# First layer's feed-forward input as seven products of halves per gate/up pair, with the output product in groups of three tiles

## Chip, cores and metric

One NeuronCore of a Trainium2 chip. The metric is the device time of one execution in microseconds (us); three executions of the kernel before are the yardstick. All numbers below come from these times, from one profiled execution of the kernel before, and from the order of its instructions on each engine.

Engines: PE is TensorE (matmul), DVE VectorE, ACT ScalarE, POOL GpSimd, SP the queue from which all transfers are issued.

## What is computed

A two-layer backbone on 512 latent and 256 context tokens, 1024 channels wide. Each layer has three mixers, a gated merge, and a SwiGLU feed-forward block; the second layer's context tokens are not needed after its mixers, so its feed-forward block sees 512 tokens, the first layer's 768.

```python
def swiglu(h, w_in, w_out):
    gate, up = jnp.split(h @ w_in, 2, axis=-1)
    return (jax.nn.silu(gate) * up) @ w_out

for l in range(DEPTH):                       # DEPTH = 2, D_MODEL = 1024, FFN_HIDDEN = 2816
    ...
    hf = rmsnorm(x, norm_ffn[l]) * (1.0 + sc_f) + sh_f
    x = x + gt_f * swiglu(hf, w_ffn_in[l], w_ffn_out[l])
    if not last:
        hfc = rmsnorm(xc, norm_ffn[l]) * (1.0 + scc_f) + shc_f
        xc = xc + gtc_f * swiglu(hfc, w_ffn_in[l], w_ffn_out[l])
```

## The kernel before

Activations lie channel-first: a tile is 128 channels by 768 tokens (512 latent, then 256 context). Every float32 operand of a large matmul is split in a high part (a cast to the matmul's float32r type) and a low part (the rest), and a product is the sum of three passes: high by high, high by low, low by high (`gemm`, `sub`). A 1024-channel input is eight k-tiles, so one block of 128 output channels costs 8 x 3 matmuls of 512 columns (latent) and as many of 256 (context).

Weights come in blocks of 128 output channels. `run_items` keeps a list of items in program order, and for each one that has a weight block it loads the block (`load`, three buffers `wr`, L300), lets ACT cast the high part (`wh`, L323) and DVE subtract to get the low part (`wl`, L326), about one to two items ahead of the matmuls. Generators that are added with `add` (norms, and `ada_late`, which computes the second layer's adaLN vectors on DVE from 256 KB pieces `wad` at L513 and L515) are advanced by `tick` between matmuls. A scheduler then sets the final order on each engine, and each engine runs its own list strictly in order.

The feed-forward block is `ffn_items`. 22 pairs of a gate and an up block; each pair is two items. The gate product is evacuated by ACT with Silu (L1616), the up product is multiplied to it by DVE straight out of PSUM (L1620), and the result is split by ACT (L173) and DVE (L174). The pairs go in groups of 8, 8 and 6; after each group the output product (w_fo, 8 blocks) takes the group's tiles as k-tiles, and DVE adds it, scaled, to the residual (L1601). The first two pairs of layer 0 are done token set by token set, since the norm of the context tokens comes later. The last group's output product goes token set by token set, with the next norm behind it.

Pools: `base` holds 27 tiles "T" (16 of them the input's high and low parts, 8 the residual), the phase's pool has 23 tiles "T2". PSUM has three banks "g" and four "h" for products.

Of the kernel before, what the change touches and what calls it, by code (L numbers as in the profile page):

```python
# [22 lines left out]
KT = D // 128  # L23
# [8 lines left out]
ZS = ((13, 19), (10, 18))  # L32
LEVELS = (1, 2, 4, 8, 16, 32, 64)
FFN_GROUPS = ((0, 8), (8, 8), (16, 6))


AQ, AK, AV, GQ, GK, GV, GR, NQ, NK, NV = 0, 4, 5, 6, 8, 10, 14, 18, 22, 26
# [90 lines left out]


class Item:  # L130
    def __init__(self, fn, w=None, nk=0, raw=False):
        self.fn, self.w, self.nk, self.raw = fn, w, nk, raw


class Net:
    def __init__(self, ctx, tc, a, out, dbg=None):
        self.ctx, self.tc, self.nc, self.a, self.out = ctx, tc, tc.nc, a, out
        self.dbg = dbg
        self.items = []
# [149 lines left out]

    def run_items(self):  # L290

        ws = [n for n, it in enumerate(self.items) if it.w is not None]
        raw, split, early = {}, {}, set()
        st = {"d": 0, "s": 0, "q": 0, "lo": None}

        def load():
            while st["d"] < len(ws) and len([q for q in raw if q not in early]) < 3:
                it = self.items[ws[st["d"]]]
                t = self.base.tile([128, 1024], F32, tag="wr", name=self.nm("wr"), bufs=3)
                self.nc.sync.dma_start(t[:, :it.nk * 128], it.w)  # L300
                raw[st["d"]] = t
                st["d"] += 1

        def split_lo():
            f, st["lo"] = st["lo"], None
            if f:
                f()

        def split_hi(k):

            while st["s"] < len(ws) and st["s"] <= k:
# [10 lines left out]
                r = raw[q]  # L322
                self.nc.scalar.copy(hi[:, :n], r[:, :n])  # L323

                def lo_part(q=q, n=n, hi=hi, lo=lo, r=r):
                    self.nc.vector.tensor_tensor(out=lo[:, :n], in0=r[:, :n], in1=hi[:, :n].bitcast(F32), op=ALU.subtract)  # L326
                    del raw[q]
                    split[q] = (hi, lo)
                st["lo"] = lo_part
                st["s"] += 1  # L330
# [18 lines left out]
        self.preload = preload  # L349
        self.ahead, self.split_lo = ahead, lambda: (split_lo(), load())  # L350
        for it in self.items:
            if it.w is None:
                it.fn()
                continue
            q = st["q"]
            load()
            if not it.raw:
                split_lo()
                if q not in split:
                    split_hi(q)  # L360
# [1127 lines left out]
    def merge_items(self, l, x_src, ntok):  # L1488
        nc = self.nc
# [117 lines left out]
    def ffn_items(self, l, ntok):  # L1607
        nc = self.nc
# [23 lines left out]
        for gi, (t0, tn) in enumerate(FFN_GROUPS):  # L1632
# [5 lines left out]
            if lead and l < DEPTH - 1:  # L1638
                self.do(lambda: self.add(self.ada_late(l + 1)))
            for t in range(t0 + lead, t0 + tn):  # L1640
                pair(t, subs_of)
            w = lambda j: self.a["w_fo"][l, j][:, t0 * 128:(t0 + tn) * 128]
            if gi < len(FFN_GROUPS) - 1:
# [148 lines left out]
```

## Time and profile before

| what | value |
|---|---|
| median of 3 executions | 2516.41 us (2516.09 to 2519.16) |
| profiled execution, device time | 2517.52 us |
| its span, first to last instruction | 2515.7 us |
| mean granted TensorE clock | 0.993 |
| PE / DVE / ACT / POOL busy, share of span | 97% / 59% / 41% / 14% |

The span is 1.8 us shorter than the profiled execution's own time, which is 1.1 us above the median. A page of the profile gives busy time by engine, the span in slices, the chain of work that ended last, and the costliest groups of instructions. Matmuls overlap at their ends, so their rate is read from the distance between starts and not from their durations; the same holds, by a few hundredths of a microsecond, for DVE.

### The profile page before, as it was taken

The numbers are of one execution on the slowest core, as the hardware profiler recorded it, in microseconds if no ns is written. First come the engines' busy times: TensorE is split into PE (matmuls) and PEld (weight loads), VectorE is DVE, ScalarE is ACT, GpSimd is POOL, SyncE is SP. The second block draws the span as 40 slices with busy tenths as digits, with TensorE's granted clock in tenths as the row PEclk, the third lists the DMA queues.
The fourth block names the chain that finished last, engine by engine and source line by source line (L and its number), as shares of the span: only waits on it lengthen the run. The fifth ranks groups of instructions, "written<-read, shape, count | busy, mean of one in ns | idle before, by whom it ended". The sixth has DMA issues, their size and how long they took to land. (4 is left out here: it accounts for less than half of the span.)

```text
span 2515.7 us, 39662 instructions
## 1 busy us (share of the span) xinstructions
PE 2441.8 (97%) x15356; PEld 2068.8 (82%) x15356; DVE 1484.7 (59%) x3006; ACT 1043.1 (41%) x1723; POOL 345.9 (14%) x442
## 2 busy tenths in 40 slices
PE   6999999999999999999999998999999999999998
PEld 3777888988878888888888876777888879988887
DVE  5675457647667673544544587757657668533336
ACT  3543345546554452212212255535545656422223
POOL 1231113204203010000000011313212220000000
PEclk9999999999999999999999999999999999999999
DMA  6433542222247333323333351223332366433334
GB/s 233 137 128 116 180 125 82 86 82 61 68 146 257 126 118 96 122 93 103 123 94 104 122 172 64 89 97 112 102 92 74 106 225 190 149 99 94 96 93 122
DMA packets 123340, 300.53 MB, mean 119 GB/s; under 512 B 22288, under 2 KB 32272, under 8 KB 123152
## 3 DMA queue, kind: packets, MB, share of 16 engines
q1 hardware_dynamic: 123152, 298.00, 37.5%
q8 instruction: 121, 1.98, 0.3%
q14 instruction: 67, 0.55, 0.1%
HBM read 258.61 MB, written 29.57 MB: 115 GB/s over the span
## 5 line engine op out<-in xcount | busy, mean ns | idle before, releaser
L211 PE MATMUL g<-T,wh 128*128 128x512 f32 (+1 forms) x4672 | 1240.1, 353 | 2.8 <-ACT T L767 2.6
L211 PEld LDWEIGHTS g<-T,wh 128*128 128x128 f32 x4672 | 801.9, 190 | 118.4 <-issue 13.6
L211 PE MATMUL g<-T,wl 128*128 128x512 f32 (+1 forms) x2336 | 814.9, 349 | 0.4 <-DVE wl L326 0.4
L211 PE MATMUL h<-T,wh 128*128 128x512 f32 (+1 forms) x2624 | 660.2, 342 | 8.5 <-ACT T L168 7.4
L323 ACT CAST wh<-wr 128x1024 fp32r<-128x1024 f32 (+2 forms) x355 | 344.6, 972 | 688.3 <-PE h L211 258.5
L326 DVE TENSOR_TENSOR wl<-wr,wh 128x1024 fp32r<-128x1024 f32 (+2 forms) x355 | 406.8, 1146 | 300.4 <-ACT wh L323 286.4
L211 PEld LDWEIGHTS h<-T,wh 128*128 128x128 f32 x2624 | 450.9, 189 | 75.7 <-ACT T L168 9.1
L211 PEld LDWEIGHTS g<-T,wl 128*128 128x128 f32 x2336 | 443.2, 190 | 57.5 <-issue 0.6
L211 PE MATMUL h<-T,wl 128*128 128x512 f32 (+1 forms) x1312 | 446.1, 340 | 2.9 <-DVE wl L326 2.9
L211 PEld LDWEIGHTS h<-T,wl 128*128 128x128 f32 x1312 | 248.1, 189 | 33.1 <-DVE wl L326 3.7
L1316 ACT ACTIVATE P<-P,sm 128x513 f32<-128x513 f32 (+3 forms) x160 | 115.9, 725 | 127.2 <-DVE sm L1358 115.9
L1321 POOL TENSOR_SCALAR P<-P,sm 128x512 f32<-128x512 f32 (+1 forms) x160 | 113.6, 712 | 366.0 <-DVE sm L1320 336.1
L515 DVE SCALAR_TENSOR_TENSOR wac<-wad,cpad,wac 128x512 f32<-128x512 f32 x168 | 119.1, 747 | 24.1 <-DMA wad<-in_w_ada_dram 23.8
L699 POOL TENSOR_TENSOR T<-T,T 128x256 f32<-128x256 f32 (+1 forms) x24 | 30.5, 1294 | 746.1 <-DVE T L1601 542.3
L1371 DVE TENSOR_TENSOR ptl<-s,pth 128x512 fp32r<-128x512 f32 (+1 forms) x144 | 107.9, 749 | 39.1 <-ACT pth L1370 37.9
L1370 ACT CAST pth<-s 128x512 fp32r<-128x512 f32 (+1 forms) x144 | 90.6, 629 | 48.6 <-PE s L215 43.5
L215 PE MATMUL s<-k_ident,P 128*128 128x128 f32 x640 | 94.1, 274 | 3.6 <-POOL P L1321 2.0
L173 ACT CAST T<-T 128x512 fp32r<-128x512 f32 (+1 forms) x93 | 49.2, 536 | 106.3 <-DVE T L1620 99.0
L1601 DVE SCALAR_TENSOR_TENSOR T<-h,mod,T 128x256 f32<-128x256 f32 (+1 forms) x67 | 40.0, 597 | 85.6 <-PE h L211 85.5
L215 PEld LDWEIGHTS s<-k_ident,P 128*128 128x128 f32 x640 | 74.3, 140 | 19.2 <-issue 5.9
L967 POOL TENSOR_TENSOR E<-E,T 128x512 f32<-128x512 f32 (+1 forms) x42 | 57.4, 1380 | 207.0 <-ACT E L963 163.6
L211 PE MATMUL o<-pth,V 128*128 128x512 f32 (+2 forms) x224 | 72.4, 332 | 0.2
(210 smaller groups left out, 2283.3 us busy)
## 6 DMA issues: line engine op xcount, KB each, us to landing
wr<-in_w_fi_dram SPq DMA_DIRECT2D x98, 512.0 KB, 3.5
wr<-in_w_in_dram SPq DMA_DIRECT2D x65, 512.0 KB, 3.7
wr<-in_w_merge_dram SPq DMA_DIRECT2D x48, 512.0 KB, 3.8
wad<-in_w_ada_dram SPq DMA_DIRECT2D x96, 256.0 KB, 3.0
wr<-in_w_ada_dram SPq DMA_DIRECT2D x32, 512.0 KB, 4.2
wr<-in_w_out_dram SPq DMA_DIRECT2D x32, 512.0 KB, 3.5
wr<-in_w_fo_dram SPq DMA_DIRECT2D x32, 512.0 KB, 3.5
wr<-in_w_br_dram SPq DMA_DIRECT2D x48, 256.0 KB, 3.0
```

The costliest lines, as they stand in the source:

```text
L173: self.nc.scalar.copy(hi, src)
L211: return self.nc.tensor.matmul(out, lhsT, rhs, **kw)
L215: return self.nc.tensor.transpose(out, src, self.ident)
L323: self.nc.scalar.copy(hi[:, :n], r[:, :n])
L326: self.nc.vector.tensor_tensor(out=lo[:, :n], in0=r[:, :n], in1=hi[:, :n].bitcast(F32), op=ALU.subtract)
L515: nc.vector.scalar_tensor_tensor(out=acc[:, s], in0=w, scalar=c, in1=acc[:, s], op0=ALU.mult, op1=ALU.add)
L967: P.tensor_tensor(out=ee[:, 1, c0:c1], in0=ee[:, 1, c0:c1], in1=self.gk[p][:, t0:t0 + c1 - c0], op=ALU.mult)
L1316: nc.scalar.activation(out=P_[:, o0:e1], in_=P_[:, o0:e1], func=AF.Exp, bias=nm_, accum_out=rz)
L1321: nc.gpsimd.tensor_scalar(out=P_[:, o0:o1], in0=P_[:, o0:o1], scalar1=rz, scalar2=1.0, op0=ALU.mult, op1=ALU.mult)
L1370: nc.scalar.copy(hi, src)
L1371: return lambda: VE.tensor_tensor(out=lo, in0=src, in1=hi.bitcast(F32), op=ALU.subtract)
L1601: self.nc.vector.scalar_tensor_tensor(out=x[:, c0:c1], in0=ps[:, :c1 - c0], scalar=self.mod[l][:, sec * 8 + j, s:s + 1], in1=x[:, c0:c1], ...
```

## The change

For the 19 pairs 3 to 21 of layer 0, a gate block G and an up block U are taken together. The 1024 input channels are cut in two halves of four k-tiles, the 768 tokens in two halves of 384, and the four products of halves per block (eight for the pair) are replaced by seven products of sums, in the variant of Strassen's scheme with shared sums.

- `combine`: once, after the third pair, it forms four sums of halves of the input (per pair of k-tiles: POOL and DVE add and subtract, ACT casts high parts, DVE three and POOL one low part), kept as 12 "T2" tiles. One sum replaces the second half of k-tiles 0 to 3, whose original halves are not needed behind it.
- `seven`: a pair is now four items, i1 (G as it is, two products), i2 (`ta`, a sum of G and U, two products), i3 (half of U and half of `tb`, two products), i4 (half of `tb`, one product). POOL forms `ta` and `tb` with four subtractions of 512 columns (line 483 of the changed kernel), after U has landed. A product is 4 k-tiles x 3 passes x 384 columns.
- Evacuation of the seven products: five additions on DVE that read PSUM, two copies on ACT, two additions and two multiplications on POOL, two Silu and two high parts on ACT, two low parts on DVE.
- The groups are seven instead of three (six of three tiles, one of four); the first item of the next group's first pair runs ahead of a group's output product.
- The phase's pool has 20 "T2" tiles instead of 23, and one buffer each for `ta` and `tb`. G's and U's buffers are held until their sums are done.

Layer 1 keeps the pairs and the groups of 8, 8 and 6.

```diff
+SEVEN_GROUPS = ((0, 3), (3, 3), (6, 3), (9, 3), (12, 3), (15, 3), (18, 4))
+SEVEN = range(3, 22)
+SEVEN_LAYERS = (0,)
...
+                if len({id(t) for q, t in raw.items() if q not in early} | {id(t) for t in self.held}) > 2:
+                    break
...
-                n = it.nk * 128
+                parts = it.parts() if it.parts else [(raw[q], 0, it.nk * 128)]
+                if parts is None:
+                    return
...
+    def combine(self, l, h2):
...
+        for i in range(4):
+            (ih, il), (jh, jl) = self.h[i], self.h[4 + i]
+            a, b = self.T(tag=self.tt), self.T(tag=self.tt)
+            P.tensor_tensor(out=a[:, m], in0=f(ih[:, m]), in1=f(il[:, m]), op=ALU.add)
+            V.tensor_tensor(out=b[:, m], in0=f(jh[:, m]), in1=f(jl[:, m]), op=ALU.add)
+            yield 2.0
...
+            V.tensor_tensor(out=b[:, m2], in0=a[:, m2], in1=b[:, m2], op=ALU.add)
+            P.tensor_tensor(out=a[:, m2], in0=a[:, m1], in1=a[:, m2], op=ALU.subtract)
+            V.tensor_tensor(out=a[:, m1], in0=b[:, m2], in1=a[:, m1], op=ALU.subtract)
+            P.tensor_tensor(out=b[:, m1], in0=b[:, m1], in1=a[:, m1], op=ALU.subtract)
+            yield 1.0
...
+            for n, ((hi, lo), o, x, w) in enumerate(pairs):
+                nc.scalar.copy(hi[:, o], x[:, w])
+            yield 1.5
+            for n, ((hi, lo), o, x, w) in enumerate(pairs):
+                (V, V, P, V)[n].tensor_tensor(out=lo[:, o], in0=x[:, w], in1=f(hi[:, o]), op=ALU.subtract)
+            yield 0.5
...
+                sub(ta[:, :512], U[:, :512], G[:, :512])
+                sub(ta[:, 512:], U[:, 512:], ta[:, :512])
...
+                sub(tb[:, :512], U[:, 512:], U[:, :512])
+                sub(tb[:, 512:], G[:, 512:], g["ta"][:, 512:])
...
+            for k in range(4):
+                xh, xl = (x[:, c(k)] for x in tiles(k))
+                s = slice(o + k * 128, o + k * 128 + 128)
+                for i, (y, x) in enumerate(((wh, xh), (wh, xl), (wl, xh))):
+                    self.matmul(ps, y[:, s], x, start=k == 0 and i == 0, stop=k == 3 and i == 2)
...
+        def i3(wh, wl):
+            p, s = g["p"], g["s"]
+            ps = product((wh, wl), 512, lambda k: self.s3[k // 2], lambda k: (m1, m2)[k % 2])
+            V.tensor_tensor(out=s[:, m2], in0=p[:, m1], in1=ps, op=ALU.add)
+            P.tensor_tensor(out=p[:, m1], in0=p[:, m1], in1=p[:, m2], op=ALU.add)
+            P.tensor_tensor(out=p[:, m2], in0=p[:, m2], in1=s[:, m2], op=ALU.add)
+            self.tick()
+            ps = product((wh, wl), 0, lambda k: self.s24[k], second)
+            V.tensor_tensor(out=p[:, m1], in0=p[:, m1], in1=ps, op=ALU.add)
+            evac(0, s, p)
...
-            self.ph = self.phx.enter_context(self.tc.tile_pool(name=f"mrg{l}", bufs=23))
+            self.ph = self.phx.enter_context(self.tc.tile_pool(name=f"mrg{l}", bufs=20))
...
+            def evac(x, s, u):
+                w = (slice(0, h2), slice(h2, ntok))[x]
+                nc.gpsimd.tensor_tensor(out=s[:, w], in0=s[:, w], in1=u[:, w], op=ALU.mult)
...
+            if by_seven and gi == 0:
+                self.do(lambda: self.add(self.combine(l, ntok // 2)))
+            if t0 + tn in by_seven:
+
+                begun = self.cap(lambda: seven(t0 + tn))
+                self.items.append(begun.pop(0))
```

Lines of the changed kernel that the order below names: L350 low part of a weight block (L326 before), L184 low part of a result (L174), L547, L555, L564, L569 and L576 the five additions out of PSUM, L444, L449, L451 and L461 DVE's share of `combine`, L483 POOL's sums of weights, L565 and L566 POOL's additions, L1830 POOL's multiplication, L706 and L708 the adaLN sums (L513 and L515), L1813 the plain pair's multiplication (L1620).

DVE, around one pair in the middle of the layer-0 feed-forward block, before: 6 rows for a pair (`wl` is the low part of a weight block, `h` and `g` are PSUM banks, the others are activation tiles).

```order
L1620 TENSOR_TENSOR T_10184<-T_10184,g_10216 128x512
L174 TENSOR_TENSOR T_10249<-T_10184,T_10248 128x512
L1620 TENSOR_TENSOR T_10184<-T_10184,h_10255 128x256
L326 TENSOR_TENSOR wl_10298<-wr_10109,wh_10297 128x1024
L174 TENSOR_TENSOR T_10249<-T_10184,T_10248 128x256
L326 TENSOR_TENSOR wl_10365<-wr_10182,wh_10364 128x1024
```

DVE, the second pair of a group of three, in the changed kernel, its second half:

```order
L708 SCALAR_TENSOR_TENSOR wac_12596<-wad_12594,cpad,wac_12596 128x512 x2
L757 TENSOR_TENSOR mod_80<-o_12580,bada_728 128x16
L350 TENSOR_TENSOR wl_12592<-wr_12369,wh_12591 128x1024
L708 SCALAR_TENSOR_TENSOR wac_12596<-wad_12651,cpad,wac_12596 128x512
L564 TENSOR_TENSOR T_12532<-T_12517,g_12584 128x384
L708 SCALAR_TENSOR_TENSOR wac_12596<-wad_12651,cpad,wac_12596 128x512
L708 SCALAR_TENSOR_TENSOR wac_12596<-wad_12705,cpad,wac_12596 128x512
L569 TENSOR_TENSOR T_12517<-T_12517,h_12611 128x384
L708 SCALAR_TENSOR_TENSOR wac_12596<-wad_12705,cpad,wac_12596 128x512
L350 TENSOR_TENSOR wl_12638<-ta_12484,wh_12637 128x1024
L184 TENSOR_TENSOR T_12627<-T_12532,T_12626 128x384
L576 TENSOR_TENSOR T_12532<-T_12532,h_12629 128x384
```

The low part of the next pair's `ta` (the row with `ta_12484`) now stands behind two additions that wait for products, and the adaLN sums stand between them.

POOL, which had no row in this stretch before, for two pairs of the changed kernel:

```order
L565 TENSOR_TENSOR T_9892<-T_9892 128x384
L566 TENSOR_TENSOR T_9892<-T_9892,T_9907 128x384
L1830 TENSOR_TENSOR T_9907<-T_9907,T_9892 128x384
L483 TENSOR_TENSOR ta_10346<-wr_10301,wr_10219 128x512
L483 TENSOR_TENSOR ta_10346<-wr_10301,ta_10346 128x512
L1830 TENSOR_TENSOR T_9907<-T_9907,T_9892 128x384
L483 TENSOR_TENSOR tb_10414<-wr_10301 128x512
L483 TENSOR_TENSOR tb_10414<-wr_10219,ta_10346 128x512
```

Eight rows per pair; the next pair's sums stand between this pair's two multiplications.

DVE at the start of `combine`, behind the third pair, in the changed kernel:

```order
L444 TENSOR_TENSOR T_9880<-T_9234,T_9235 128x768
L1813 TENSOR_TENSOR T_9765<-T_9765,h_9836 128x256
L449 TENSOR_TENSOR T_9880<-T_9879,T_9880 128x384
L350 TENSOR_TENSOR wl_9873<-wr_9724,wh_9872 128x384
L184 TENSOR_TENSOR T_9834<-T_9765,T_9833 128x256
L451 TENSOR_TENSOR T_9879<-T_9880,T_9879 128x384
L461 TENSOR_TENSOR T_9174<-T_9880,T_9173 128x384
```

The sums of the input are threaded between the third pair's last multiplication and the low parts of the first output product's blocks; nothing of them stands earlier on DVE.

## Rows read from the trace of the kernel before

**Rows 1.** The page, part 1: busy time and share of each engine.

```profile
PE 2441.8 (97%) x15356; PEld 2068.8 (82%) x15356; DVE 1484.7 (59%) x3006; ACT 1043.1 (41%) x1723; POOL 345.9 (14%) x442
```

**Rows 2.** Windows, 960 to 1400 us, layer 0's pairs: window, length, PE, PEld, DVE, ACT, POOL, clock.

```profile
960.00:1400.00 440.00, 440.00 (x2637) 383.98 (x2637) 213.01 (x308) 89.52 (x133) 0.00 (x0) 1.00 0.33 105
```

**Rows 3.** Timeline of PE: one product of a block, 512 then 256 columns; start, length.

```profile
1104.60 0.62 PE L211 MATMUL h<-T,wh 128*128 128x512 f32 x2
...
1110.19 0.40 PE L211 MATMUL h<-T,wh 128*128 128x256 f32 x2
...
1112.92 0.62 PE L211 MATMUL g<-T,wh 128*128 128x512 f32 x2
```

**Rows 4.** Timeline of PE in layer 0's attention: four matmuls of 384 columns, then 256.

```profile
379.54 0.34 PE L211 MATMUL o<-pth,V 128*128 128x384 f32 x1
...
380.25 0.28 PE L211 MATMUL o<-pth,V 128*128 128x256 f32 x1
```

**Rows 5.** Timeline of DVE within a pair, back to back, 1155 to 1159 us.

```profile
1155.28 0.69 DVE L174 TENSOR_TENSOR T<-T,T 128x512 fp32r<-128x512 f32 x1
1155.88 1.41 DVE L515 SCALAR_TENSOR_TENSOR wac<-wad,cpad,wac 128x512 f32<-128x512 f32 x2
1157.21 0.41 DVE L1620 TENSOR_TENSOR T<-T,h 128x256 f32<-128x256 f32 x1
1157.54 1.22 DVE L326 TENSOR_TENSOR wl<-wr,wh 128x1024 fp32r<-128x1024 f32 x1
1158.67 0.42 DVE L174 TENSOR_TENSOR T<-T,T 128x256 fp32r<-128x256 f32 x1
```

**Rows 6.** Timeline of DVE in an output product: the residual's additions, 512 and 256 columns.

```profile
1433.04 0.75 DVE L1601 SCALAR_TENSOR_TENSOR T<-h,mod,T 128x512 f32<-128x512 f32 x1 [0.57 <-PE h L211]
1433.72 0.96 DVE L326 TENSOR_TENSOR wl<-wr,wh 128x768 fp32r<-128x768 f32 x1
...
1467.47 0.48 DVE L1601 SCALAR_TENSOR_TENSOR T<-h,mod,T 128x256 f32<-128x256 f32 x1 [0.56 <-PE h L211]
1467.88 0.15 DVE L190 SCALAR_TENSOR_TENSOR nsm<-nsm 128x4 f32<-128x4 f32 x1
```

**Rows 7.** POOL's two-input operations: 512 columns (by form, 779 to 830 us), 384 (timeline).

```profile
L1576 POOL TENSOR_TENSOR T<-T,T 128x512 f32<-128x512 f32 x8 | 10.3, 1292 | 69.2 <-DVE T L1574 64.5 <-ACT T L1512 3.2 <-issue 1.2
...
1753.86 1.01 POOL L1307 TENSOR_TENSOR X<-X,k_maskc 128x384 f32<-128x384 f32 x1
```

**Rows 8.** Timeline of POOL and DVE at layer 0's end (next norm), 1473 to 1480 us.

```profile
1473.61 5.14 POOL L699 TENSOR_TENSOR T<-T,T 128x512 f32<-128x512 f32 x3 [542.32 <-DVE T L1601]
...
1474.34 1.53 DVE L629 TENSOR_TENSOR T<-T,T 128x256 f32<-128x256 f32 x1
1475.80 3.50 DVE L692 SCALAR_TENSOR_TENSOR T<-T,gain,T 128x512 f32<-128x512 f32 x2
1479.22 0.47 DVE L1601 SCALAR_TENSOR_TENSOR T<-g,mod,T 128x256 f32<-128x256 f32 x1
```

**Rows 9.** Timeline of POOL and DVE in layer 0's merge, 787 to 792 us.

```profile
787.37 5.01 POOL L1576 TENSOR_TENSOR T<-T,T 128x512 f32<-128x512 f32 x4 [3.24 <-ACT T L1512]
...
787.84 1.38 DVE L326 TENSOR_TENSOR wl<-wr,wh 128x512 fp32r<-128x512 f32 x1 [0.28 <-ACT wh L323]
789.14 0.68 DVE L1574 TENSOR_TENSOR T<-T,h 128x512 f32<-128x512 f32 x1
...
790.58 1.21 DVE L326 TENSOR_TENSOR wl<-wr,wh 128x512 fp32r<-128x512 f32 x1
```

**Rows 10.** The adaLN sums of layer 1: operations on tile wac, and what they waited for.

```profile
L515 DVE SCALAR_TENSOR_TENSOR wac<-wad,cpad,wac x168: 732/747/755, 745.5 to 1520.7; 128x512 f32<-128x512 f32 x168
...
  DMA wad<-in_w_ada_dram: 23.8, 23
```

**Rows 11.** Timeline of PE at the end of layer 0's merge: matmuls that waited for DVE.

```profile
909.54 0.38 PE L211 MATMUL h<-T,wl 128*128 128x256 f32 x1 [1.21 <-DVE wl L326]
...
913.84 0.39 PE L211 MATMUL h<-T,wl 128*128 128x256 f32 x1 [1.31 <-DVE wl L326]
```

More of the change, by code (lines that the diff above doesn't have):

```diff
@@ L130, with __init__ @@
 class Item:
-    def __init__(self, fn, w=None, nk=0, raw=False):
+    def __init__(self, fn, w=None, nk=0, raw=False, got=None, parts=None, done=None):
         self.fn, self.w, self.nk, self.raw = fn, w, nk, raw
+        self.got, self.parts, self.done = got, parts, done
+        self.weights = w is not None or parts is not None
 class Net:
@@ L142, in __init__ @@
         self.late = []
+        self.held, self.todo, self.sumt = [], deque(), {}
         self.begun = False
@@ L290, in run_items @@
     def run_items(self):
-        ws = [n for n, it in enumerate(self.items) if it.w is not None]
+        ws = [n for n, it in enumerate(self.items) if it.weights]
         raw, split, early = {}, {}, set()
@@ L296, in load @@
         def load():
-            while st["d"] < len(ws) and len([q for q in raw if q not in early]) < 3:
+            while st["d"] < len(ws):
                 it = self.items[ws[st["d"]]]
+                if it.w is None:
+                    raw[st["d"]] = None
+                    early.add(st["d"])
+                    st["d"] += 1
+                    continue
+                if len({id(t) for q, t in raw.items() if q not in early} | {id(t) for t in self.held}) > 2:
+                    break
                 t = self.base.tile([128, 1024], F32, tag="wr", name=self.nm("wr"), bufs=3)
@@ L301, in load @@
                 raw[st["d"]] = t
+                if it.got:
+                    it.got(t)
                 st["d"] += 1
@@ L307, in split_lo @@
                 f()
+            self.sums()
         def split_hi(k):
+            self.sums()
             while st["s"] < len(ws) and st["s"] <= k:
@@ L318, in split_hi, with lo_part @@
                     return
-                n = it.nk * 128
+                parts = it.parts() if it.parts else [(raw[q], 0, it.nk * 128)]
+                if parts is None:
+                    return
                 hi = self.base.tile([128, 1024], F32R, tag="wh", name=self.nm("wh"), bufs=3)
                 lo = self.base.tile([128, 1024], F32R, tag="wl", name=self.nm("wl"), bufs=3)
[L322 to L326, printed above, removed]
+                for r, c, n in parts:
+                    self.nc.scalar.copy(hi[:, c:c + n], r[:, :n])
+                def lo_part(q=q, it=it, parts=parts, hi=hi, lo=lo):
+                    for r, c, n in parts:
+                        self.nc.vector.tensor_tensor(out=lo[:, c:c + n], in0=r[:, :n],
+                                                     in1=hi[:, c:c + n].bitcast(F32), op=ALU.subtract)
                     del raw[q]
+                    if it.done:
+                        it.done()
                     split[q] = (hi, lo)
@@ L351, in run_items @@
         for it in self.items:
-            if it.w is None:
+            if not it.weights:
                 it.fn()
@@ L395, in gemm @@
         self.items.append(Item(fn, w, nk))
+    def combine(self, l, h2):
+        nc = self.nc
+        V, P = nc.vector, nc.gpsimd
+        f = lambda x: x.bitcast(F32)
+        m1, m2, m = slice(0, h2), slice(h2, 2 * h2), slice(0, 2 * h2)
+        self.s24, self.s3 = [], []
+        self.acc = None
+        for i in range(4):
[4 more added lines that the diff above has]
+            yield 2.0
+            self.s24.append((self.T(F32R, "T2"), self.T(F32R, "T2")))
+            if i % 2 == 0:
+                self.s3.append((self.T(F32R, "T2"), self.T(F32R, "T2")))
+            V.tensor_tensor(out=b[:, m2], in0=a[:, m2], in1=b[:, m2], op=ALU.add)
[3 more added lines that the diff above has]
+            yield 1.0
+            x3 = (m1, m2)[i % 2]
+            pairs = [(self.s24[i], m1, a, m1), ((ih, il), m2, b, m2), (self.s3[i // 2], x3, a, m2),
+                     (self.s24[i], m2, b, m1)]
+            for n, ((hi, lo), o, x, w) in enumerate(pairs):
[4 more added lines that the diff above has]
+            yield 0.5
+        self.ready.add(("S", l))
@@ L1640, in ffn_items @@
             for t in range(t0 + lead, t0 + tn):
-                pair(t, subs_of)
+                if t in by_seven:
+                    self.items += begun or self.cap(lambda: seven(t))
+                    begun = []
+                else:
+                    pair(t, subs_of)
+            if by_seven and gi == 0:
[3 more added lines that the diff above has]
+                self.items.append(begun.pop(0))
             w = lambda j: self.a["w_fo"][l, j][:, t0 * 128:(t0 + tn) * 128]
-            if gi < len(FFN_GROUPS) - 1:
+            if gi < len(groups) - 1:
                 for j in range(8):
```

102 lines of the change are left out of this document (101 added, 1 removed).

## Prediction

> **What bounds the kernel now.** First the page's busy times: PE is busy for 97% of the span, DVE 59%, ACT 41%, POOL 14% [rows 1]. A share over the whole span says little of one stage, so next the windows over layer 0's pairs: in 440 us PE is busy for all 440, at the full clock (1.00, the 2.4 GHz level), DVE for 213, ACT for 90, POOL for nothing [rows 2]. There only matmul time counts, and what is taken from PE shortens the kernel, as long as no other engine comes to need more time than PE. So the question is put to each engine: how much work does it get per pair, against how much PE time is left?
>
> **What PE gains.** One block takes 24 matmuls of 512 and 24 of 256 columns. They start at 1104.60 and the next block's at 1112.92, 8.32 us [rows 3], so a pair is 16.64 us. A changed pair is 7 products x 4 k-tiles x 3 passes = 84 matmuls of 384 columns; the changed order has 19 x 84 = 1596 of them. Their rate: four of 384 columns in the attention take 380.25 - 379.54 = 0.71 us, 0.1775 each [rows 4]; halfway between 512 (5.59 / 24 = 0.233) and 256 (2.73 / 24 = 0.114) is 0.173 [rows 3]. I take 0.175, since the attention's rows stand among other shapes and these don't: 84 x 0.175 = 14.70 us. Gain 1.94 us a pair, 19 pairs 36.9 us; ends 32.9 (at 0.1775) and 39.9 (at 0.173). The output product keeps its matmuls in number and size: 8 blocks x 3 tiles = 3/8 x 8.32 = 3.12 us each, 25.0 us a group of three.
>
> **What DVE and POOL get.** From starts of rows that follow back to back [rows 5]: a low part of 1024 columns 1.13 us, a two-input operation of 512 columns 0.60, of 256 columns 0.33, so 0.47 at 384; an adaLN sum 1.33 / 2 = 0.67. The residual's additions are 0.68 and 0.41 [rows 6]. POOL takes 1.29 us at 512 and 1.01 at 384 [rows 7], so some 1.85 at 768 by the same slope.
> A changed pair on DVE: low parts 1.13 + 1.13 + 3 x 0.60 = 4.06, results' low parts 2 x 0.47 = 0.94, additions out of PSUM 5 x 0.47 = 2.35: 7.35 us. Before it was 2 x 1.13 + 2 x 0.60 + 2 x 0.33 = 4.1. On POOL: 4 x 1.29 + 4 x 1.01 = 9.2 us, before nothing. Each fits in 14.7 us by itself. ACT's casts grow from 2048 to 3584 columns on an engine that is busy for a fifth [rows 2]: costed at nothing, DVE's and POOL's work covers it; without that cover it would be 1.6 us a pair.
>
> **What decides: DVE and POOL do not run side by side.** While POOL runs three operations of 512 columns (5.14 us), DVE's 256-column operation takes 1.53 us instead of 0.41, and two of 512 take 3.50 instead of 1.4 [rows 8]. In the merge a low part of 512 columns takes 1.38 and 1.21 beside POOL, but an operation that reads a product in PSUM keeps its 0.68 [rows 9]. So two-input work from SBUF on DVE and POOL's work add up, and only DVE's additions out of PSUM overlap with POOL.
> A group (three pairs and the output product) then has: PE 3 x 14.70 + 25.0 = 69.1 us. DVE 3 x 7.35 = 22.1, output product 8 x (0.47 + 0.68 + 0.41) = 12.5, adaLN sums: the order puts 144 of all 192 between the first and the last changed pair, 144 x 0.67 / 6.3 groups = 15.2 [rows 5, 10]; together 49.8. POOL 27.6. DVE and POOL: 77.4 us, of which 3 x 2.35 + 8 x 1.09 = 15.8 read PSUM. So between 61.6 us (all of those overlap with POOL) and 77.4 (none), against PE's 69.1. In the pairs POOL has work for about half the time and waits for its turn on top, so I take 0.6 of 7.1; in the output product it has 5.2 us of sums in 25, so a quarter of 8.7: 6.4 us overlap, 71.0 us, 1.9 over PE. Splits run one to two items ahead (some 6 us), which evens out the pairs that carry adaLN sums, not a lack that each group repeats. 6.3 groups x 1.9 = 12 us lost.
>
> **The input's sums, once.** On DVE they start behind the third pair's last multiplications (order of DVE). POOL has 4 x (1.85 + 3 x 1.01) = 19.5 us, less the first addition, that nothing holds back, plus three weight sums: 21.6. DVE has 4 x (0.87 + 5 x 0.47) = 12.9 and, threaded in, 8 low parts of the output product and one of `ta`, 4.9. Of the 39.4 us together, PE covers 0.7 + 4.2 (i1) + 25.0 = 29.9 us before i2 needs the sums. PE waits for about 10 us; ends 6 and 16 (none of the output product's 8.7 us of residual additions overlaps).
>
> **Edits with one answer.** Loads: same bytes, smaller blocks for the output product; cover, the two items that they are ahead. Three "T2" tiles fewer can delay the norm ahead of the block, where PE already waits 1.2 to 1.3 us for DVE twice [rows 11]: 0 to 3 us in each of two layers. The adaLN sums' last 14 operations now follow the next norm in one piece: 0 to 5 us, where DVE already waits for their loads at times (23.8 us in 23 waits over the kernel [rows 10]). I take 1 us for both.
>
> **Sum.** 2517.5 (the profiled execution's own time, 1.8 us over its span, 1.1 over the median of the runs shown) - 36.9 + 12 + 10 + 1 = 2503.6. Forecast **2503.5 us**.
>
> **A rule beside it.** The Trainium skill, GPSIMD Engine Reference, section "Engine selection", sends elementwise work of two inputs to VectorE, GpSimd being about half as fast, and its table of measured times gives a ratio of 1.96. The rows here give 1.29 / 0.60 = 2.15. By the page's ratio a POOL pair would be an estimated 8.4 us for 9.2, a group 68.6 us, below PE, and the sum 2491.6; the rows decide.
>
> **Rivals.**
> *Hidden after all.* If POOL's work falls mostly beside DVE's additions out of PSUM (over 8.3 of 15.8 us a group), a group stays under 69.1 us, and only the input's sums cost, some 7 us: 2517.5 - 36.9 + 7 = 2488. For it: DVE's waits for products leave POOL free stretches. Against: the adaLN sums fill them in the order.
> *A balance.* With 3.5 us lost in a group (22 us) and the rest as above, 2514; within 0.2%, about what a measurement of this kernel can tell from no change (2511.4 to 2521.4).
> *Slower: DVE and POOL become the bound.* If none of the overlap comes about, a group takes 77.4 us, 8.3 over PE: 52 us, with 16 for the input's sums and 5 for the end of the layer 2517.5 - 36.9 + 73 = 2554. The place is the second pair of a group: DVE 7.35, some 6 adaLN sums 4.0, POOL 9.2, 20.6 us for 14.7 of PE, and DVE in strict order, where the low part of the next `ta` stands behind additions that wait for products. It decides from 36.9 - 11 = 25.9 us, 4.1 a group, under 4.2 us of overlap. For it: a matmul waits as soon as one low part is late [rows 11]. The Trainium skill, SBUF — State Buffer, section "Who interferes with whom", says that a vector instruction with two SBUF inputs and a GpSimd instruction that reads SBUF exclude each other for the whole instruction, and that one with a single SBUF input does not; the trace agrees (1.53 us for 0.41 [rows 8], 0.68 unchanged [rows 9]).
> *It does not do what it says.* If a matmul of 384 columns took as long as 0.195 us, PE would gain 0.3 us a pair, and the time be about 2535; the order shows the 1596 matmuls and rows 4 their rate, so 0.02.
>
> **Chances.** The forecast's case (2493 to 2511) 0.37, hidden 0.20, balance 0.17, slower 0.24, not as it says 0.02. Faster by over 0.2%: 0.57; within: 0.17; slower: 0.26. Range 2484 to 2540: the low end takes in the hidden case down to a gain of 39.9 us with 6 for the sums, the high end two thirds of the way to no overlap; one in ten lies on each side. The likeliest case has its own range, 2493 to 2511.
>
> **What would show it.** Right: starts of 384-column matmuls 0.173 to 0.178 us apart; PE idle for some 10 us once, before the first product of the input's sums, released by DVE's low parts or ACT's casts; in the windows over the pairs PE near 97%, DVE and POOL busy times (which count waiting for each other) well above 7.35 and 9.2 us a pair; waits of PE ended by DVE L350. Wrong: PE idle under 10 us in the whole block (hidden), over 35 us (slower), or waits of PE ended by transfers or by PSUM evacuation instead of low parts.

## The result, and the profile after

The changed kernel takes 2559.05 us (median of 4, 2554.79 to 2560.89); the kernel before, on the same chip, 2516.31. The ratio is 1.0165, with a 95% interval of 1.0147 to 1.0182: slower by about 42 us, where 2503.5 was forecast, and 19 us above the upper end of the range. The profiled execution took 2560.89 us, its span 2559.1, at a mean granted clock of 0.983 (before 0.993).

The page's busy times of the changed kernel, to set beside [rows 1]:

```profile
PE 2429.3 (95%) x15128; PEld 2076.6 (81%) x15128; DVE 1667.7 (65%) x3240; ACT 1104.6 (43%) x1866; POOL 591.3 (23%) x610
```

Windows of the changed kernel, all of them inside layer 0's pairs (window, length, PE, PEld, DVE, ACT, POOL, clock). The second holds the larger part of the sums of the input, which run from 975 to 1015 us, and the first two changed pairs behind them:

```profile
1060.00:1450.00 390.00, 365.61 (x2145) 338.15 (x2143) 312.81 (x437) 118.84 (x214) 174.77 (x124) 0.99 0.34 105
```

```profile
985.00:1050.00 65.00, 54.29 (x290) 47.72 (x289) 62.80 (x75) 19.81 (x36) 42.89 (x30) 0.93 0.31 97
```

Before, PE was busy for all 440 us [rows 2]. Now it stands for 24 of 390, and in the second window for 11 of 65. The full clock is gone too: 0.99 and 0.93 for 1.00.

What it waits for, 930 to 1500 us (engine, line waited for: us in total, times, longest):

```profile
PE g L221 <- DVE wl L350: 17.4, 10, 3.5
PE h L221 <- DVE wl L350: 8.9, 8, 3.1
PE g L221 <- ACT T L183: 7.3, 2, 3.8
PE h L221 <- ACT T L183: 2.0, 2, 1.7
...
```

PE waits for low parts of weights, and in four places for the high part of a group's last result. Of the L350 waits 10.4 us lie between 985 and 1050: 4.1 up to the first product of the input's sums, which goes on at 1013.06 us, and 6.4 behind it, in two waits for the low parts of the next gate blocks. The last operation of the sums is POOL's at 1014.14; in front of the first of these low parts DVE has three adaLN sums:

```profile
1013.06 0.44 PE L221 MATMUL h<-T,wl 128*128 128x384 f32 x1 [0.66 <-DVE wl L350]
...
1014.14 1.33 POOL L461 TENSOR_TENSOR T<-T,T 128x384 fp32r<-128x384 f32 x1
...
1022.56 3.68 DVE L708 SCALAR_TENSOR_TENSOR wac<-wad,cpad,wac 128x512 f32<-128x512 f32 x3
1026.17 1.21 DVE L350 TENSOR_TENSOR wl<-wr,wh 128x1024 fp32r<-128x1024 f32 x1
```

PE's timeline at this wait (start, length, operation, [idle before <- releaser]):

```profile
1021.85 0.51 PE L221 MATMUL g<-T,wh 128*128 128x384 f32 x2
1022.20 0.33 PE L221 MATMUL g<-T,wl 128*128 128x384 f32 x1
1022.37 0.51 PE L221 MATMUL g<-T,wh 128*128 128x384 f32 x2
...
1027.43 0.69 PE L221 MATMUL g<-T,wl 128*128 128x384 f32 x1 [3.51 <-DVE wl L350]
1027.92 0.84 PE L221 MATMUL g<-T,wh 128*128 128x384 f32 x2
1028.56 0.52 PE L221 MATMUL g<-T,wl 128*128 128x384 f32 x1
1028.88 0.84 PE L221 MATMUL g<-T,wh 128*128 128x384 f32 x2
```

Ahead of the wait three matmuls take 0.52 us, 0.173 each. Behind it three take 0.96, 0.32 each: the clock record has 1.2 GHz from 1027.1 to 1030.5 us, and this costs in addition to the 3.51 us.

Two more places, outside the pairs. The start of the block, which answers to [rows 11], and the end of layer 0:

```profile
921.89 0.79 PE L221 MATMUL g<-T,wl 128*128 128x512 f32 x1 [4.49 <-DVE wl L350]
...
1559.93 1.32 PE L221 MATMUL g<-wac,sel 128*32 128x128 f32 x16 [12.16 <-DVE wac L708]
```

The last sums of adaLN (`wac`) are 12.16 us late for the matmul that reads them.

**Where the time lies.** Three marks can be found in every kernel's timeline: the first Silu of layer 0's gate products (with the load of its table), the end of layer 0's last addition to the residual, and the first such addition of layer 1. They cut the time from the first to the last operation on the engines, some 3.6 us less than the page's span, into lead, block, boundary and rest. Lengths in us; "idle" is PE's, "half" the time that the clock record shows at 1.2 GHz, idle time included. From the third line on they are the experiments.

| kernel | lead | block (idle, half) | boundary (idle, half) | rest |
|---|---|---|---|---|
| before | 922.7 | 570.3 (2.2, 0) | 601.3 (16.4, 10.2) | 417.8 |
| after | 930.7 | 586.6 (42.1, 27.3) | 617.0 (28.7, 13.7) | 421.2 |
| groups_only | 930.5 | 569.9 (5.1, 3.2) | 611.2 (18.3, 13.9) | 420.0 |
| last6 | 926.7 | 571.4 (3.5, 3.4) | 606.6 (18.6, 17.1) | 420.8 |
| t2_20 | 931.4 | 569.6 (2.5, 0) | 602.3 (19.4, 6.8) | 420.4 |
| held_blocks | 927.5 | 586.0 (11.3, 13.7) | 599.6 (17.5, 3.4) | 417.2 |
| all_dve | 927.4 | 535.6 (8.0, 10.8) | 623.6 (26.9, 33.5) | 418.9 |
| wsum_dve | 927.6 | 570.1 (30.2, 23.9) | 617.9 (28.1, 20.5) | 419.3 |
| rest_dve | 931.3 | 550.0 (17.2, 10.2) | 618.9 (26.8, 23.9) | 419.8 |
| pool_beside | 927.5 | 595.6 (49.2, 47.1) | 619.1 (28.7, 17.7) | 420.5 |
| ada_thin | 928.2 | 546.6 (18.0, 11.7) | 609.5 (17.3, 8.8) | 420.1 |
| pace | 927.6 | 597.3 (50.1, 44.4) | 605.5 (16.6, 3.4) | 419.0 |
| dve_pace_l1 | 931.5 | 535.9 (10.1, 10.1) | 604.9 (15.6, 3.6) | 418.1 |

Up to 840 us nothing is changed, yet the profiled executions lie up to 5 us apart there by the clock at their start (after 3.4 us behind before). The change's own loss is read from the block and what follows.

### The profile page after: what moved, and what is told of

The parts are those of the page before. It is cut to its first block, busy times and chain, and to the rows that moved or that the text cites. A ratio compares the mean times of both kernels' runs of the same rounds, so it can differ in the third digit from the quotient of the medians.

```text
span 2559.1 us, 40070 instructions
## 1 busy us (share of the span) xinstructions
PE 2429.3 (95%) x15128; PEld 2076.6 (81%) x15128; DVE 1667.7 (65%) x3240; ACT 1104.6 (43%) x1866; POOL 591.3 (23%) x610
## 5 line engine op out<-in xcount | busy, mean ns | idle before, releaser
L221 PE MATMUL g<-T,wh 128*128 128x512 f32 (+2 forms) x4588 | 1227.9, 354 | 11.8 <-ACT T L183 7.3
L221 PEld LDWEIGHTS g<-T,wh 128*128 128x128 f32 x4588 | 795.3, 191 | 123.0 <-issue 17.5
L221 PE MATMUL g<-T,wl 128*128 128x512 f32 (+2 forms) x2294 | 802.8, 350 | 21.9 <-DVE wl L350 21.9
L221 PE MATMUL h<-T,wh 128*128 128x512 f32 (+2 forms) x2556 | 660.8, 345 | 11.6 <-ACT T L178 7.7
L346 ACT CAST wh<-wr 128x1024 fp32r<-128x1024 f32 (+3 forms) x387 | 341.3, 883 | 577.4 <-PE g L221 205.3
L350 DVE TENSOR_TENSOR wl<-wr,wh 128x1024 fp32r<-128x1024 f32 (+3 forms) x387 | 413.6, 1069 | 213.9 <-ACT wh L346 199.0
L221 PE MATMUL h<-T,wl 128*128 128x512 f32 (+2 forms) x1278 | 439.7, 344 | 9.2 <-DVE wl L350 8.9
L708 DVE SCALAR_TENSOR_TENSOR wac<-wad,cpad,wac 128x512 f32<-128x512 f32 x168 | 149.4, 913 | 10.5 <-DMA wad<-in_w_ada_dram 10.1
L183 ACT CAST T<-T 128x512 fp32r<-128x512 f32 (+2 forms) x93 | 49.3, 538 | 153.4 <-POOL T L1830 140.0
L1794 DVE SCALAR_TENSOR_TENSOR T<-h,mod,T 128x512 f32<-128x512 f32 (+1 forms) x98 | 59.0, 608 | 57.1 <-PE h L221 56.5
L892 POOL TENSOR_TENSOR T<-T,T 128x256 f32<-128x256 f32 (+1 forms) x24 | 29.9, 1271 | 245.5 <-issue 92.6
L184 DVE TENSOR_TENSOR T<-T,T 128x512 fp32r<-128x512 f32 (+2 forms) x93 | 58.1, 632 | 35.8 <-ACT T L183 35.3
```

The costliest lines, as they stand in the source:

```text
L184: self.late.append((lo, lambda: self.nc.vector.tensor_tensor(out=lo, in0=src, in1=hi.bitcast(F32), op=ALU.subtract)))
L221: return self.nc.tensor.matmul(out, lhsT, rhs, **kw)
L346: self.nc.scalar.copy(hi[:, c:c + n], r[:, :n])
L350: self.nc.vector.tensor_tensor(out=lo[:, c:c + n], in0=r[:, :n], in1=hi[:, c:c + n].bitcast(F32), op=ALU.subtract)
L708: nc.vector.scalar_tensor_tensor(out=acc[:, s], in0=w, scalar=c, in1=acc[:, s], op0=ALU.mult, op1=ALU.add)
L1794: self.nc.vector.scalar_tensor_tensor(out=x[:, c0:c1], in0=ps[:, :c1 - c0], scalar=self.mod[l][:, sec * 8 + j, s:s + 1], in1=x[:, c0:c1], ...
```

## Experiments

**All of POOL's new work on DVE (all_dve).**

In `combine`, in the sums of weights, in i3 and in the evacuation:

```diff
-        V, P = nc.vector, nc.gpsimd
+        V, P = nc.vector, nc.vector
...
-            sub = lambda o, x, y: nc.gpsimd.tensor_tensor(out=o, in0=x, in1=y, op=ALU.subtract)
+            sub = lambda o, x, y: nc.vector.tensor_tensor(out=o, in0=x, in1=y, op=ALU.subtract)
...
-            P.tensor_tensor(out=p[:, m1], in0=p[:, m1], in1=p[:, m2], op=ALU.add)
-            P.tensor_tensor(out=p[:, m2], in0=p[:, m2], in1=s[:, m2], op=ALU.add)
+            V.tensor_tensor(out=p[:, m1], in0=p[:, m1], in1=p[:, m2], op=ALU.add)
+            V.tensor_tensor(out=p[:, m2], in0=p[:, m2], in1=s[:, m2], op=ALU.add)
...
-                nc.gpsimd.tensor_tensor(out=s[:, w], in0=s[:, w], in1=u[:, w], op=ALU.mult)
+                nc.vector.tensor_tensor(out=s[:, w], in0=s[:, w], in1=u[:, w], op=ALU.mult)
```

> POOL's new work in the layer-0 feed-forward block (sums of weights, the two additions in i3, the multiplication, POOL's share of the input's sums) is done by DVE; nothing else differs. Theory A (DVE's two-input work from SBUF and POOL's work take turns, so low parts of weights come late): a group then has 49.8 + 12 x 0.60 + 12 x 0.47 = 62.6 us of DVE work against 69.1 us of PE and no turns to wait for. PE's idle time between 930 and 1500 us falls from some 39 us to under 15, the half-clock stretches that follow its stalls become fewer, and the time goes from 2559 to 2510 to 2535 us. The wait of 12 us for the adaLN sums behind the block stays. Rival B (DVE has too much in its strict order, whoever does POOL's part): 12.8 us more on DVE per group make the low parts later still: PE's idle time above 45 us, 2562 to 2590 us.

2511.15 us, ratio 0.9968 (0.9956 to 0.9979). DVE has 168 operations more on the page (3408 for 3240), yet its busy time grows by 9.5 us alone (1677.2 for 1667.7), and the block is 51 us shorter than in the changed kernel; the boundary, with the wait for the adaLN sums and more time at half clock, takes 6.6 us of that back. Its window over the pairs:

```profile
1060.00:1450.00 390.00, 389.58 (x2343) 366.10 (x2342) 358.55 (x629) 140.60 (x245) 0.00 (x0) 1.00 0.42 125
```

DVE is busy for 92% of the time and PE for all of it. B falls: a DVE that is busy for 92% and runs in strict order does no harm here. The stretching is seen by comparing DVE's groups, same shapes, 1060 to 1450 us (busy, mean ns | idle before, releaser), first the changed kernel:

```profile
L708 DVE SCALAR_TENSOR_TENSOR wac<-wad,cpad,wac 128x512 f32<-128x512 f32 x112 | 102.9, 941 | 4.6 <-DMA wad<-in_w_ada_dram 4.4 <-DVE wl L350 0.2
L350 DVE TENSOR_TENSOR wl<-tb,wh 128x512 fp32r<-128x512 f32 x30 | 27.1, 904 | 0.0
...
L350 DVE TENSOR_TENSOR wl<-ta,wh 128x1024 fp32r<-128x1024 f32 x15 | 23.7, 1582 | 11.8 <-ACT wh L346 11.8
L184 DVE TENSOR_TENSOR T<-T,T 128x384 fp32r<-128x384 f32 x30 | 20.4, 679 | 24.4 <-ACT T L183 24.2
...
L706 DVE TENSOR_SCALAR wac<-wad,cpad 128x512 f32<-128x512 f32 x16 | 13.9, 906 | 0.5 <-PE h L221 0.5
...
L569 DVE TENSOR_TENSOR T<-T,h 128x384 f32<-128x384 f32 x12 | 6.6, 548 | 6.9 <-POOL T L565 6.9
```

then all_dve:

```profile
L708 DVE SCALAR_TENSOR_TENSOR wac<-wad,cpad,wac 128x512 f32<-128x512 f32 x119 | 86.8, 749 | 3.7 <-DMA wad<-in_w_ada_dram 3.6
L350 DVE TENSOR_TENSOR wl<-tb,wh 128x512 fp32r<-128x512 f32 x32 | 22.0, 687 | 0.0
...
L350 DVE TENSOR_TENSOR wl<-ta,wh 128x1024 fp32r<-128x1024 f32 x16 | 19.5, 1221 | 0.1
...
L184 DVE TENSOR_TENSOR T<-T,T 128x384 fp32r<-128x384 f32 x32 | 17.8, 556 | 0.6 <-ACT T L183 0.6
...
L706 DVE TENSOR_SCALAR wac<-wad,cpad 128x512 f32<-128x512 f32 x16 | 7.3, 481 | 0.0
L569 DVE TENSOR_TENSOR T<-T,h 128x384 f32<-128x384 f32 x13 | 7.2, 552 | 0.3 <-PE h L221 0.2
```

Two losses show side by side. Operations with two inputs from SBUF were longer beside POOL: 112 x 0.192 + 30 x 0.217 + 15 x 0.361 + 30 x 0.123 = 37 us in the first four groups shown, while L569, which reads a product in PSUM, kept its 0.55 us. One kind of operation that reads a single tile from SBUF was longer too: L706, the first step of an adaLN sum, 906 ns for 481. And DVE stood idle for 43 us in front of three of the groups (L350 of `ta`, L184, L569), waiting for results that POOL had to make first: for the first two ACT's cast stands between, and ACT waited for POOL's multiplication in front of all 30 of its casts L183 here.

POOL's operations were longer in their turn, in the same 390 us of the changed kernel:

```profile
L483 POOL TENSOR_TENSOR tb<-wr 128x512 f32<-128x512 f32 x16 | 25.9, 1617 | 20.6 <-DVE wl L350 20.6
...
L483 POOL TENSOR_TENSOR ta<-wr,wr 128x512 f32<-128x512 f32 x16 | 21.6, 1353 | 114.5 <-DMA wr<-in_w_fi_dram 110.7 <-DVE mod L757 3.8
```

**Work on POOL whose result nothing reads (pool_beside).** On top of all_dve:

```diff
+            def beside(U):
+                for i in range(3):
+                    x = self.ph.tile([128, 344], F32, tag="sc", name=self.nm("sc"), bufs=1)
+                    nc.gpsimd.tensor_tensor(out=x, in0=U[:, :344], in1=U[:, 344:688], op=ALU.subtract)
...
                 sub(ta[:, 512:], U[:, 512:], ta[:, :512])
+                beside(U)
...
                 sub(tb[:, 512:], G[:, 512:], g["ta"][:, 512:])
+                beside(U)
```

> The kernel with all of POOL's new work on DVE, plus work on POOL whose result nothing reads: per changed pair six subtractions of 344 columns from the landed up block into a scratch tile, three behind each pair of sums of weights, an estimated 0.95 us each by the slope between POOL's 384 and 512 columns, 17 us a group. Nothing waits for these results; only the up block's buffer is held until they are read. Theory A (turns: two-input work of DVE from SBUF stands still while POOL works): DVE's operations on weights and adaLN sums are stretched as in the changed kernel, 62.6 + 17 = 80 us a group less up to 16 of overlap, against 69: 2520 to 2560 us. Rival N (what costs is only that DVE waits in strict order for results of POOL): no stretched operations and 2507 to 2515 us, as without this work.

2567.66 us, ratio 1.0186 (1.0169 to 1.0203), 56 us above all_dve and 8 us above the upper end of A's own 2520 to 2560: A has the sign right and the price too low, POOL's operations taking 1.27 us each for the estimated 0.95. N falls. That the up block's buffer is held longer is not the cause: DVE's sums of weights waited 2.2 us for loads in the window below, in all_dve 4.7. The windows of pool_beside over the pairs, and two of its groups on DVE and POOL's own:

```profile
1060.00:1450.00 390.00, 359.81 (x2091) 334.57 (x2090) 366.93 (x545) 117.33 (x209) 120.65 (x96) 0.97 0.34 102
```

```profile
L350 DVE TENSOR_TENSOR wl<-tb,wh 128x512 fp32r<-128x512 f32 x29 | 27.4, 944 | 0.0
...
L483 DVE TENSOR_TENSOR ta<-wr,ta 128x512 f32<-128x512 f32 x16 | 19.8, 1235 | 0.0
...
L488 POOL TENSOR_TENSOR sc<-wr 128x344 f32<-128x344 f32 x96 | 121.6, 1267 | 291.4 <-DMA wr<-in_w_fi_dram 284.9
```

The same low part of 512 columns takes 944 ns beside POOL and 687 without; PE stands again. This is the rule of the Trainium skill, SBUF — State Buffer, section "Who interferes with whom", at the size of a whole stage, and the trace agrees with it: 904 and 944 ns for 687 with two inputs from SBUF, 548 and 552 with one input from SBUF and one from PSUM. The section frees instructions with a single SBUF input only outside the two-port modes, which `tensor_scalar` can enter; the prediction left that condition out. L706 is such an operation (906 ns for 481), but no run here shows the mode it ran in.

**Half of POOL's work moved (wsum_dve, rest_dve).** The first moves only `sub` of the diff above to DVE, the second all but `sub`.

> Of POOL's new work only the four sums of weights per pair go to DVE; the additions in i3, the multiplications and POOL's share of the input's sums stay on POOL (4 x 1.01 us a pair). Theory A (turns, all of POOL's work counts alike): per group DVE 49.8 + 7.2 = 57.0 and POOL 12.1, together 69.1 less some overlap, about PE's own 69.1: most of the gain of the run with all work on DVE, 2511 to 2528 us. Rival F (only the tail matters: multiplication on POOL, then cast, then low part, before the output product): the waits of PE for casts and low parts of results stay, 2530 to 2550 us.

> The other half: sums of weights stay on POOL (4 x 1.29 us a pair), all else of POOL's new work goes to DVE. Theory A: per group DVE 49.8 + 5.6 = 55.4 and POOL 15.5, together 70.9 less some overlap, a little more than the run before this one: 2515 to 2535 us. Rival F (the tail matters, not the sums): as the run with all work on DVE, 2508 to 2514 us. Rival G (the sums of weights at the head of the chain are what makes low parts late): most of the loss stays, 2540 to 2555 us.

wsum_dve: 2540.14 us, ratio 1.0087 (1.0072 to 1.0102). rest_dve: 2522.35, ratio 1.0012 (1.0001 to 1.0023). A alone fits the second and misses the first by 12 us; F alone fits the first and misses the second by 8 us. With only 12 us of POOL work left in a group, but that at the end of the chain, 29 of the 48 us stayed that lie between all_dve and the changed kernel. In wsum_dve, 1060 to 1450 us:

```profile
L184 DVE TENSOR_TENSOR T<-T,T 128x384 fp32r<-128x384 f32 x33 | 18.4, 556 | 20.4 <-ACT T L183 20.0
```

DVE still waits 20 us for the cast that follows POOL's multiplication, with low parts of weights queued behind it. So F holds beside A: POOL costs by its turns, and again where DVE's strict order waits for it. Which part of the 29 us is which was not separated.

**The adaLN sums (ada_thin, pace).**

First the edit of ada_thin, then that of pace:

```diff
-            for s in range(2):
+            for s in range(2 if kt < 2 else 0):
...
-            yield 4.5
+            yield 4.0
```

> The changed kernel with 6 of 8 adaLN sums left out (second layer's vectors are computed from two of eight k-tiles; the loads stay), so DVE has some 11.4 us less in a group and no tail of sums behind the block. Theory A or B (DVE with its turns against POOL is the bound, 77.4 us a group against 69.1): 66 us fit under PE; PE's idle time between 930 and 1500 us falls under 15 us, the wait behind the block goes: 2500 to 2520 us. Rival E (latency: sum on POOL, cast on ACT, low part on DVE, one behind another behind a load, whatever DVE's load): idle time stays over 30 us, only the wait of 12 us goes: 2540 to 2550 us.

> The adaLN sums are paced with 4.0 us between two steps instead of 4.5, so that they end inside the block although it has less PE time; the same operations. Theory C (with 37 us less PE time in the block the sums no longer fit at their old pace, their tail stands alone behind the block, and PE waits 12.2 us for it at 1560 us): that wait goes, with the half-clock stretch of 13.7 us around it: 2538 to 2549 us. Rival: the sums, now closer together, put 0.5 / 4.5 more of their work into each pair, DVE is later there by some 1.7 us a group, and 6 to 10 us of the 12 come back as waits for low parts: 2550 to 2558 us.

ada_thin leaves out six of eight sums and so does not compute the second layer's vectors. It takes 2506.84 us, ratio 0.9952 (0.9937 to 0.9967): with less on DVE the turns fit, and E falls. PE's idle time between 930 and 1500 us is 18.3 us where under 15 was expected; over 7 of them are waits for the next layer's norm. pace: 2554.04, ratio 1.0141 (1.0126 to 1.0156), above C's 2549 and in the rival's range. The wait at the boundary goes as C says (idle 28.7 to 16.6 us), but the block becomes 10.7 us longer: here, on a DVE that has no room beside POOL, an operation moved in is paid for.

**Groups, tiles.** groups_only is the plain pairs in the changed kernel's groups (with the result tiles counted from the group's first pair); last6 is groups_only with six tiles in the last group, and so six groups for seven; t2_20 is the kernel before with 20 "T2" tiles. Their edits in this order:

```diff
-SEVEN = range(3, 22)
+SEVEN = ()
...
-SEVEN_GROUPS = ((0, 3), (3, 3), (6, 3), (9, 3), (12, 3), (15, 3), (18, 4))
+SEVEN_GROUPS = ((0, 3), (3, 3), (6, 3), (9, 3), (12, 4), (16, 6))
...
-            self.ph = self.phx.enter_context(self.tc.tile_pool(name=f"mrg{l}", bufs=23))
+            self.ph = self.phx.enter_context(self.tc.tile_pool(name=f"mrg{l}", bufs=20))
```

> The plain pairs of the kernel before with layer 0's groups of three tiles and 20 T2 tiles: no products of halves, no sums. Theory A: groups cost DVE 32 more rounds of additions (35 us over the block, beside PE) and PE nothing by their size; the output product of a group starts right behind its last pair, so up to 1 to 2 us a group for its last tile: 2518 to 2532 us. Rival D (the short groups are what costs, by the chain from the last pair's result to the output product and by additions into the residual): at least half of the 36 us of idle time shows here too: 2535 to 2560 us.

> As the kernel with groups alone, but the last group has six tiles as in the kernel before (3, 3, 3, 3, 4, 6). Theory H (the last group's output product of four tiles is 8 x 2 x 3 x 0.114 = 5.5 us shorter in the context tokens' part, so the next layer's norm has that much less cover and PE waits for it): 8 to 11 us of the 16 us that groups alone cost go, 2525 to 2529 us. Rival: the loss is in the many short output products or in the 20 T2 tiles: 2533 to 2538 us.

> The kernel before with 20 T2 tiles for 23 in both layers, nothing else. Theory M (the fewer tiles hold the norm ahead of the feed-forward block back, in both layers): the 1.2 and 1.3 us that PE waits there become one wait of 4.5 us with a half-clock stretch in layer 0, 4 us in all, and 2 us in layer 1: 2521 to 2525 us. Rival (the wait at the block's start comes from the change behind it, by what the scheduler moves ahead): 2516 to 2519 us.

groups_only: 2536.12 us, ratio 1.0065 (1.0048 to 1.0082). The number is 4 us above A's range and lies in D's, but D is wrong: the block is as short as before (569.9 us, 5.1 idle). What costs is 10 us at the boundary and, with the fewer tiles, some 4 us in front of the block and 2 in the rest. last6: 2529.85, ratio 1.0043 (1.0028 to 1.0058); the intervals overlap, and of H's 8 to 11 us 4.6 show at the boundary, and the block gives 1.5 of them back. Its time lies between H's range and the rival's, and what makes up the rest at the boundary is open. t2_20: 2523.97, ratio 1.0021 (1.0011 to 1.0030), and the wait ahead of the block is 4.50 us as in the changed kernel: M holds.

**Late blocks in the kernel before (held_blocks).**

`late` is the number of repeats for the six blocks, 0 for all others.

```diff
                 r = raw[q]
+                for _ in range(it.late):
+                    self.nc.vector.tensor_scalar(out=r[:, :512], in0=r[:, :512], scalar1=1.0, scalar2=None, op0=ALU.mult)
```

> The kernel before, in which six weight blocks of layer 0's feed-forward block (gate blocks of pairs 4, 6, 10, 12, 14, 18) come late on purpose: before their split, DVE multiplies half of the raw block by 1.0 in place 30, 34, 38, 42, 46 and 54 times, 0.41 us each by the rows of single-input operations. No products of halves, no work of POOL, the same matmuls. Theory K (the clock falls because PE stood still): PE waits at some of the six places for the block's high or low part, 2 to 12 us each, and beside each of the longer waits a stretch at half clock stands that the kernel before has not; the time grows by more than PE's idle time, by 1.7 us for each 3.4 us at half clock: with some 20 us idle, 2540 to 2550 us. Rival L (the half-clock stretches of the changed kernel come from its matmuls of 384 columns or from DVE and POOL together, not from the waits): no half-clock stretch in the pairs, and the time grows by the idle time alone, within 2 us.

2534.48 us, ratio 1.0060 (1.0045 to 1.0075). PE waited at two of the six places, 5.12 and 3.96 us, and beside each stands a stretch of 6.8 us at 1.2 GHz; the kernel before has none in this block. PE's timeline at the first, 512-column matmuls:

```profile
1233.40 1.65 PE L213 MATMUL g<-T,wh 128*128 128x512 f32 x4 [5.12 <-ACT wh L327]
...
1236.14 0.63 PE L213 MATMUL g<-T,wl 128*128 128x512 f32 x1
1236.56 1.06 PE L213 MATMUL g<-T,wh 128*128 128x512 f32 x2
1237.42 0.63 PE L213 MATMUL g<-T,wl 128*128 128x512 f32 x1
...
1240.18 0.62 PE L213 MATMUL g<-T,wh 128*128 128x512 f32 x2
1240.64 0.40 PE L213 MATMUL g<-T,wl 128*128 128x512 f32 x1
1240.87 0.62 PE L213 MATMUL g<-T,wh 128*128 128x512 f32 x2
```

1.28 us for three matmuls just behind the wait, 0.69 from 1240 on. The block grew by 15.7 us: 9.1 us of idle time and 6.6 more, which is 13.7 us at half speed (6.8). No POOL, no 384 columns: K's mechanism holds and L falls. K's 2540 to 2550 us were for some 20 us of idle time, and PE waited for 9.1.

**The pieces together (dve_pace_l1):** all_dve, the pace of 4.0, and `bufs=20 if l == 0 else 23`.

> All of POOL's new work on DVE, the adaLN sums paced with 4.0 us for 4.5, and 23 T2 tiles again in layer 1. Theory C with A: DVE has room in the block without turns (some 63 us of 69 a group), so the closer sums come back as nothing, the wait of 12.1 us behind the block goes together with the half-clock stretch of 17 us beside it, and layer 1's feed-forward block starts 2.5 us sooner: 2490 to 2500 us. Rival: DVE, then busy for over 92% of the block, is late again and gives back 6 us or more: 2502 to 2510 us.

2500.17 us, ratio 0.9921 (0.9906 to 0.9936): faster than both kernels, some 20 us under the one before, at the upper edge of the range expected. The wait for adaLN is gone (idle at the boundary 26.9 to 15.6 us, half clock 33.5 to 3.6), the block did not grow, the rest is short again. Left are the 4 us ahead of the block and a wait of 6.3 us for the next layer's norm behind the last group.

## Why the prediction was wrong

- **PE's gain held.** Matmuls start 0.173 us apart where 0.175 was taken: 84 x 0.1735 = 14.57 us a pair, 39.3 us in all for 36.9. all_dve, where little else is lost, has a block 34.7 us shorter.
- **The input's sums were priced too high.** About 10 us of idle time were forecast before the first product of the sums; there PE waited 4.3 us, ended by L350 but for 0.2. The sums' length was right, 40 us on DVE (974.7 to 1014.6) for 39.4, but PE had 34 us of other work before that product went on, for 29.9. That the window from 985 to 1050 us has 10.6 in all is luck: the other 6.4 stand behind the sums, at the low parts of the next two pairs' gate blocks. DVE had no idle time between 1011.8 and 1047.3 us, so these can be arrears of the sums or the pairs' own lack; no run separates the two.
- **The step that failed: "6.4 us overlap, 71.0 us, 1.9 over PE", 12 us lost.** The mechanism was right: turns of DVE and POOL make low parts late. The price was not. Between 1013 and 1500 us, behind the sums of the input, PE idled 32.5 us, 5.2 a group for 1.9, or 26.1 and 4.1 without the two waits just named (the block's 42.1 less 4.3 before 1013 and 5.3 at its end, for the next layer's norm). The sum added work and left out order. DVE also stands still in its strict order, 43 of 390 us in three kinds of operations, while it waits for POOL's part of a result; and POOL's operations are longer in their turn, 1.35 to 1.62 us each for 1.29 at 512 columns [rows 7]. A group's DVE time is thus not 49.8 us plus a share of POOL's. wsum_dve and rest_dve show the same: 12.1 us of POOL's work in a group (as their expectations count it), at the chain's end, cost 29 us over all_dve, and 15.5 us, at its head, cost 11. How much the splits that run ahead evened out, no run shows.
- **"I take 1 us for both" was mis-sized.** Three "T2" tiles fewer cost about 5 us (t2_20), where 0 to 3 was given for each of two layers and a part of 1 was taken. The adaLN sums' tail was a wait of 12.16 us, where 0 to 5 was given. Their pace is set in PE time, and the block has 37 us less of it: 37 / 4.5 is eight steps, two operations each, that no longer fit, and with a pace of 4.0 the wait is gone. The text had counted the 14 operations behind the norm and not asked what PE does until they are done.
- **A term was missing: the clock.** Waits of PE bring stretches at 1.2 GHz, 41 us in block and boundary for 10 before. From the block's start to 1600 us the matmuls in them took 13.2 us more than at full clock (the distances between starts, less 0.228, 0.1735 and 0.1165 us for 512, 384 and 256 columns), before 4.5: some 9 us.
- **The sum, for block and boundary:** -39.3 + 52.2 (idle, 70.8 for 18.6) + 8.7 (clock) = 21.6, measured +32.0. Of the other 10 us some 4 come from how idle time is counted: from a matmul's end, which lies some 0.17 us behind the point at which the next one would have started. Over 35 waits from the block's start to 1600 us that makes 6.3 us, before 2.1 over 11. The rest is put down to no one cause.
- **The rival "slower", 2554 us, named the place and the sign.** That its total comes within 5 us is luck, for its terms do not stand singly: it had 52 us in the groups, 16 for the input's sums and 5 behind the block, where 32.5, 4.3 and some 16 were found, and the clock came on top. Its condition, over 25.9 us lost, was met by PE's waits alone, and so was the sign given for it, PE idle over 35 us in the block (42.1).

## What to carry to other kernels

Before giving POOL a share of DVE's work, ask whether DVE could do it alone: here, with DVE busy for 92%, PE lost 0.4 of 390 us in the pairs, while the same work on POOL stretched DVE's operations with two inputs from SBUF and put POOL's slower steps into chains that DVE's strict order waits for. Price each new wait of a saturated PE at more than its length: here the clock fell with the longer ones. And where background work is paced by another stage's time, shortening that stage moves its tail behind the end.

## Not expected of the hardware

Not forecast was how closely the clock follows PE's waits in a stage that had run at 2.4 GHz throughout: each of the seven stretches at 1.2 GHz in the changed kernel's block stands at one of its seven longest waits, 2.25 to 3.83 us. Length alone does not decide it: the next longest, 2.23 us, has none, and in all_dve one stands behind two waits of 1.0 us. In held_blocks the two waits that were made on purpose brought 6.8 us each at half clock, 0.73 us lost for each us of waiting (6.6 / 9.1). That POOL's subtraction of 344 columns takes 1.27 us beside a busy DVE, about what 512 columns take alone (1.29 [rows 7]), was not foreseen either; DVE is held up as well (944 ns for 687).
